# Two heads' scores in one step, compression without zero fills, GLA norm weights applied after the turn

## Chip, cores and metric

The kernel runs on one core of a Trainium2 chip. The metric is the device time of one execution in microseconds; the median of three runs is compared. Engines are named as in the profile: PE is TensorE's matmul, PEld its weight load, DVE VectorE, ACT ScalarE, POOL GpSimd, SP SyncE.

## What is computed

Two transformer blocks, one behind the other, on one sequence of 256 tokens with 1024 channels in fp32. The first block mixes by sparse attention (NSA) and by retention, then an MLP; the second by a state-space scan (SSD) and gated linear attention (GLA), then cross-attention to a memory of 256 rows and a SwiGLU. Cut to what the change touches:

```python
# first block, NSA: 8 heads of 64 in 2 groups, keys compressed in blocks of 32 with stride 16 (15 blocks)
blk = k[cmp_idx] + pe[None, :, None, :]
k_cmp = jax.nn.silu(blk.reshape(n_cmp, G, 32 * 64) @ w1) @ w2          # and v_cmp likewise
p_s = softmax(where(causal, q @ k_sel.T * scale, NEG));  o_s = p_s @ v_sel
p_w = softmax(where(causal, q @ k_win.T * scale, NEG));  o_w = p_w @ v_win
o = gate[..., 0] * o_c + gate[..., 1] * o_s + gate[..., 2] * o_w
# second block, GLA: 4 heads, 256 value channels each
o = rmsnorm_2(o, norm_g).reshape(Bsz, S, GLA_DV)                       # norm_g: 256 weights, same for each head
return (o * jax.nn.silu(r.astype(jnp.float32))).astype(q.dtype)
# second block, SSD: y = C (decay masks) B X, decay masks exp(cs_l - cs_s) per head
```

With 256 tokens all key blocks are selected, so the selected branch and the window branch are both plain causal attention.

## The kernel before

Weights come as 314 units of 128 x 1024 fp32 (512 KB), in the order in which the program asks for them. `load` (line 89 on) issues the transfer on SP's queue into one of 4 `raw` buffers; ACT casts it to fp32r as `wh` (line 96), DVE subtracts to get the low part `wl` (line 97); there are 8 buffers of each. A projection is then three matmuls per 128 channels: high by high, high by low, low by high (`tok_mm` for token rows, `feat_mm` for features). All matmuls go through `mm` (line 106) and all transposes through `tr` (line 110); `split` (line 113) is the cast to a high part on ACT and the subtraction to a low part on DVE.

PSUM has 8 banks in three rings: `acc` with 4, `sm` with 3, `po` with 1. SBUF tiles come from rings too: `k2` (14 buffers) holds most passing tiles, `g2` (9) the gates, values and z tiles.

`stream` is a generator of projections that aren't needed yet; `pump()` takes one piece of it and is called between the steps of the mixers, so that PE has matmuls while other engines do softmax and norms. `need` takes pieces until a result is there. The order of the program isn't the last word: the kernel is built with `schedule_with_timeline_sim=True`, so a planner with a cost for each instruction puts the instructions of each engine in an order ahead of time, and hands out the buffers and banks. On the chip each engine then works through its own list in that order, waiting on semaphores.

The places of the change, in order of time:

- `start` (line 274 on): 14 warm-up matmuls; x's first 128 rows on the SP and ACT queues (line 289); two rows of gains on POOL's queue (line 290), which PE spreads over the partitions by a product with a row of ones, for the first norm (line 318).
- `compress` (line 366 on), called for keys and then for values: four adds put the block positions on (line 374), and for each of four tiles DVE writes zeros twice into a 128-column stationary block (line 381) that takes the high part at columns 0 to 29 and the low part at 64 to 93. 32 matmuls per call, with the weights as the moving side.
- `nsa_rest` (line 610 on): blocks (m, t, i) are pairs of heads by row tile t and group i. `scores` is called for one head at a time: products with the high and the low keys of both branches into one bank, a mask product, the maximum (line 625), two exponentials with their sums (line 629), the reciprocal (631), the gate (633), two scalings (635). `turn` transposes both heads of a block, `values` multiplies with the values. With t = 0 a branch has 128 keys, with t = 1 it has 256.
- `ssd`, `decays` (line 1045 on): POOL makes the block-diagonal tile `bd` (line 1056) that PE spreads over the partitions; ACT takes the exponentials (1061), DVE multiplies with C B (1062). `products` ends a block: sum, z gate (1085), squares on ACT (1087), norm (1089).
- `silu2` (line 461 on) with `mul`: the GLA gate r times its sigmoid, then times the norm weights on POOL (line 469). `gla` (line 1148 on): masks and states, small scalings with the chunk decays (1177, 1178), and for each of four row tiles the norm and the gate (1208), and `to_T`, which transposes a tile and splits it.

Of the kernel before, what the change touches and what calls it, by code (L numbers as in the profile page):

```python
# [32 lines left out]
B_CONV, B_BA, B_DTB, B_AL, B_D, B_A2, B_N = 0, 60, 64, 80, 96, 112, 624  # L33

G_MIX, G_MLP, G_FIN, G_MIX2, G_XATT, G_MEM, G_FFN, G_FIN2, G_SSD, G_GLA, G_NUM = range(11)
# [16 lines left out]
class Builder:  # L52
# [207 lines left out]
    def to_T(self, rows, t, dst, n=8, b0=0):  # L260

        for k0 in range(0, n, 4):
            ps = self.PS()
            for j in range(4):
                self.tr(ps[:, j * P:(j + 1) * P], rows[:, (k0 + j) * P:(k0 + j + 1) * P])
            v = ps.rearrange("p (a b) -> p a b", a=4)
            ts = slice(t * P, (t + 1) * P)
            self.mark = self.split(dst.hi[b0 + k0 // 4][:, :, ts], dst.lo[b0 + k0 // 4][:, :, ts], v)
# [5 lines left out]
    def start(self):  # L274
# [91 lines left out]
    def compress(self, src, pe, w1, w2v, is_v):  # L366

        nc = self.nc
        xt = self.T("k2", [P, 16, 30])
        xv = xt.rearrange("p j (g c) -> p g c j", g=2)  # L370
        sv = src.rearrange("p g (c s) -> p g c s", s=16)
        for h in range(2):
            for g in range(2):
                nc.vector.tensor_tensor(
                    xv[:, g, :, h * 8:(h + 1) * 8], sv[:, g, h:h + 15, 0:16:2],
                    pe[:, None, h * 8:(h + 1) * 8].broadcast_to((P, 15, 8)), op=OP.add)
        xs = []
        for q in range(4):
            x = self.T("k2", [P, 4, P], F32R)
            for c in (30, 94):  # L380
                nc.vector.tensor_scalar(x[:, :, c:c + 34], self.cst[:, None, 0:34].broadcast_to((P, 4, 34)), 0.0, None, op0=OP.mult)
            self.split(x[:, :, 0:30], x[:, :, 64:94], xt[:, 4 * q:4 * q + 4])
            xs.append(x)
        ph = self.PS()
        for q in range(4):
            for j, (wh, wl) in enumerate(self.load(w1, 0, 256, 4 * q, 4)):
                x = xs[q][:, j]
# [3 lines left out]
        hs = self.T("k2", [P, 256])  # L391
        nc.scalar.copy(hs, ph[:, :256])
        pt = self.PS()
        for m in range(2):
            self.mm(pt[:, m * 30:(m + 1) * 30], hs[:, m * P:(m + 1) * P], self.cst[:, C_I94:C_I94 + 30], True, True)
# [65 lines left out]
    def silu2(self, acc, mul=None):  # L461

        out = []
        for t in range(2):
# [3 lines left out]
            if mul is not None:  # L468
                self.nc.gpsimd.tensor_tensor(x, x, mul, op=OP.mult)
# [140 lines left out]
    def nsa_rest(self, kv_, gt, pcT, vbd):  # L610
# [5 lines left out]
        def scores(m, t, i, c):  # L616
            h = 4 * i + 2 * m + c
            w = (t + 1) * P
            ps = self.PS()
            o = ps[:, :2 * w].rearrange("p (a b) -> p a b", a=2)  # L620
            for k in (khi, klo):
                self.mm(o, Q[h // 2][:, c, t * P:(t + 1) * P], k[:, i::2, 0:w], k is khi, False)
            self.mm(o[:, :, t * P:w], self.cb[:, 0], self.cb[:, 1:2].broadcast_to((P, 2, P)), False, True)
            mx = self.S(2)
            nc.vector.tensor_reduce(mx, ps[:, :2 * w].rearrange("p (a b) -> p a b", a=2), axis=AX, op=OP.max, negate=True)  # L625
            e = self.T("k2", [P, 512])
            sm = self.S(2)
            for br in range(2):
                nc.scalar.activation(e[:, br * w:(br + 1) * w], ps[:, br * w:(br + 1) * w], AF.Exp, bias=mx[:, br:br + 1], accum_out=sm[:, br:br + 1])  # L629
            rc = self.S(2)  # L630
            nc.vector.reciprocal(rc, sm)
            f = self.S(2)
            nc.vector.tensor_tensor(f, rc, gt[:, t, h, 1:3], op=OP.mult)
            for br in range(2):
                nc.vector.tensor_scalar(e[:, br * w:(br + 1) * w], e[:, br * w:(br + 1) * w], f[:, br:br + 1], None, op0=OP.mult)
            return e

        def turn(m, t, i, e):


            w = (t + 1) * P
            blocks = [(br, kb) for br in range(2) for kb in range(t + 1)]
            parts = []
            for n in range(t + 1):
                pt = self.PS()
                for a in range(2):
                    br, kb = blocks[2 * n + a]
                    for c in range(2):
                        q = (2 * a + c) * P
                        self.tr(pt[:, q:q + P], e[c][:, br * w + kb * P:br * w + (kb + 1) * P])  # L650
# [331 lines left out]
    def stream2(self, hT, pb, dec, a1T):  # L982
# [28 lines left out]
    def ssd(self, hT, pb, dts, z, dec):  # L1011
# [33 lines left out]
        def decays(g, t, q):  # L1045
# [10 lines left out]
            nc.gpsimd.tensor_tensor(bd, csT[:, t:t + 1].bitcast(F32).broadcast_to((P, 4, P)),  # L1056
# [91 lines left out]
    def gla(self, dec_):  # L1148
# [7 lines left out]
        for i in range(2):  # L1156
# [36 lines left out]
            for t in range(2):  # L1193
# [18 lines left out]
                late = [lambda o=o, t=t, i=i: self.to_T(o, t, yT, 4, i)]  # L1212
# [113 lines left out]
    def block2(self, hT, rest):  # L1326
# [7 lines left out]
        gT = self.gla(dec)  # L1334
# [18 lines left out]
def layout(inp):  # L1353
# [25 lines left out]
    for r in range(3):  # L1379
# [3 lines left out]
        A["gla_b_a_2"][0].reshape(4, P).T, rep(A["ssd_dt_bias_2"]), rep(A["ssd_A_log_2"]), rep(A["ssd_D_2"]), a2], 1)  # L1383
    D["gains"] = np.stack([A["norm_mix"][0], A["norm_mlp"][0], A["norm_final"], A["norm_mix_2"][0], A["norm_xattn_2"][0], A["norm_mem_2"][0],
                           A["norm_ffn_2"][0], A["norm_final_2"], A["ssd_norm_2"][0], np.tile(A["gla_norm_2"][0], 4)])
# [64 lines left out]
```

## Time and profile before

| | |
|---|---|
| median of 3 runs | 1002.63 us (1000.57 to 1003.64) |
| the profiled execution | 1002.8 us, its span 1001.0 us |
| instructions | 16172 |
| busy: PE, DVE, ACT, POOL | 980.6, 661.9, 510.7, 53.8 us |
| mean granted TensorE clock | 0.992 of full speed |
| from HBM | 172.81 MB, 174 GB/s over the span |

The busy shares are means over the whole kernel. Whether a step costs time is read from its own stretch: a table of windows gives, for each, how long each engine was busy, the granted clock and the share of the DMA engines. Rows of the timeline give start, duration, engine, line and operation, the tile written and the tiles read, and in brackets the idle time of the engine before it and what ended it.

### The profile page before, as it was taken

The numbers are of one execution on the slowest core, as the hardware profiler recorded it, in microseconds if no ns is written. First come the engines' busy times: TensorE is split into PE (matmuls) and PEld (weight loads), VectorE is DVE, ScalarE is ACT, GpSimd is POOL, SyncE is SP. The second block draws the span as 40 slices with busy tenths as digits, with TensorE's granted clock in tenths as the row PEclk, the third lists the DMA queues.
The fourth block names the chain that finished last, engine by engine and source line by source line (L and its number), as shares of the span: only waits on it lengthen the run. The fifth ranks groups of instructions, "written<-read, shape, count | busy, mean of one in ns | idle before, by whom it ended". The sixth has DMA issues, their size and how long they took to land.

```text
span 1001.0 us, 16172 instructions
## 1 busy us (share of the span) xinstructions
PE 980.6 (98%) x6388; PEld 876.9 (88%) x6388; DVE 661.9 (66%) x994; ACT 510.7 (51%) x797; POOL 53.8 (5%) x80
## 2 busy tenths in 40 slices
PE   8999999899999999999999989999999999999997
PEld 5878999787888899789898888998998879899995
DVE  6798768866755555678878666677756467455543
ACT  5656546635644444465765535555545345444432
POOL 1000100000000000100010231200000000000000
PEclk8999999999999999999999999999999999999999
DMA  7656744233655666276446442753755157556531
GB/s 274 213 195 223 253 138 146 87 128 126 221 190 185 200 215 195 106 251 199 155 147 190 148 148 85 253 191 128 229 190 187 45 190 248 193 169 203 177 126 42
DMA packets 49212, 174.92 MB, mean 175 GB/s; under 512 B 5984, under 2 KB 6240, under 8 KB 49136
## 3 DMA queue, kind: packets, MB, share of 16 engines
q1 hardware_dynamic: 46512, 166.15, 50.5%
q0 software_dynamic: 2192, 6.94, 2.2%
q8 instruction: 50, 0.82, 0.3%
q10 hardware_dynamic: 432, 0.79, 0.2%
q14 instruction: 26, 0.21, 0.1%
HBM read 172.81 MB, written 1.05 MB: 174 GB/s over the span
## 4 chain that ended last, share of the span: by engine, by line
PE 90%; DVE 5%; ACT 2%; DMA 2%; issue 1%; POOL 0%; POOLq 0%; ACTq 0%; DVEq 0%
PE acc L106 64%; PE sm L106 23%; PE sm L110 2%; DVE wl L97 2%; PE po L106 1%; DMA raw<-in_wbig_dram 1%; ACT wh L96 1%; DMA k<-in_gains_dram 1%; ACT hh L113 0%; DVE hl L113 0%; ACT k L629 0%; DVE k L113 0%; DVE gd L555 0%; DVE sc L625 0%; PE po L110 0%
## 5 line engine op out<-in xcount | busy, mean ns | idle before, releaser
L97 DVE TENSOR_TENSOR wl<-raw,wh 128x1024 fp32r<-128x1024 f32 (+1 forms) x314 | 379.5, 1221 | 214.7 <-ACT wh L96 213.4
L96 ACT CAST wh<-raw 128x1024 fp32r<-128x1024 f32 (+1 forms) x314 | 325.5, 1049 | 292.7 <-PE acc L106 133.7
L106 PE MATMUL acc<-hh,wh 128*128 128x256 f32 x736 | 207.2, 283 | 3.8 <-ACT g L271 3.3
L106 PE MATMUL acc<-hh,wl 128*128 128x256 f32 x736 | 207.5, 282 | 0.0
L106 PE MATMUL acc<-hl,wh 128*128 128x256 f32 x736 | 206.4, 281 | 0.0
L106 PE MATMUL acc<-wl,hh 128*128 128x512 f32 (+1 forms) x400 | 158.1, 396 | 0.7 <-DVE wl L97 0.7
L106 PE MATMUL acc<-wh,hh 128*128 128x512 f32 (+1 forms) x400 | 156.7, 397 | 1.2 <-ACT hh L113 1.1
L106 PE MATMUL acc<-wh,hl 128*128 128x512 f32 (+1 forms) x400 | 156.4, 396 | 0.0
L106 PEld LDWEIGHTS acc<-hh,wh 128*128 128x128 f32 x736 | 138.4, 189 | 5.4 <-ACT g L271 3.5
L106 PEld LDWEIGHTS acc<-hl,wh 128*128 128x128 f32 x736 | 139.1, 189 | 0.2
L106 PEld LDWEIGHTS acc<-hh,wl 128*128 128x128 f32 x736 | 139.0, 189 | 0.3 <-issue 0.2
L106 PE MATMUL sm<-hh,wl 128*128 128x256 f32 x488 | 136.5, 280 | 0.0
L106 PE MATMUL sm<-hl,wh 128*128 128x256 f32 x488 | 136.4, 279 | 0.0
L106 PE MATMUL sm<-hh,wh 128*128 128x256 f32 x488 | 136.4, 279 | 0.0
L106 PEld LDWEIGHTS sm<-hl,wh 128*128 128x128 f32 x488 | 91.7, 188 | 0.8
L106 PEld LDWEIGHTS sm<-hh,wh 128*128 128x128 f32 x488 | 91.4, 187 | 0.9
L106 PEld LDWEIGHTS acc<-wh,hh 128*128 128x128 f32 x400 | 75.7, 190 | 18.6 <-ACT hh L113 2.7
L106 PEld LDWEIGHTS acc<-wl,hh 128*128 128x128 f32 x400 | 76.0, 190 | 18.2 <-DVE wl L97 1.9
L106 PEld LDWEIGHTS sm<-hh,wl 128*128 128x128 f32 x488 | 91.6, 188 | 0.0
L106 PEld LDWEIGHTS acc<-wh,hl 128*128 128x128 f32 x400 | 75.9, 190 | 17.9 <-DVE hl L113 1.1
L106 PE MATMUL acc<-wl,gd 128*128 128x512 f32 x216 | 85.4, 396 | 0.0
L106 PE MATMUL acc<-wh,gd 128*128 128x512 f32 x216 | 85.1, 395 | 0.0
(292 smaller groups left out, 1079.4 us busy)
## 6 DMA issues: line engine op xcount, KB each, us to landing
raw<-in_wbig_dram SPq DMA_DIRECT2D x311, 512.0 KB, 4.1
k<-in_gains_dram POOLq DMA_DIRECT2D x18, 256.0 KB, 4.5
k<-in_mem_dram POOLq DMA_DIRECT2D x4, 256.0 KB, 5.6
raw<-in_wbig_dram SPq DMA_DIRECT2D x2, 420.0 KB, 3.8
k<-in_decay_dram POOLq DMA_DIRECT2D x4, 192.0 KB, 5.1
xr<-in_x_dram SPq DMA_DIRECT2D x1, 512.0 KB, 6.6
out_dram<-k SPq DMA_DIRECT2D x2, 256.0 KB, 2.5
out_dram<-k ACTq DMA_DIRECT2D x2, 256.0 KB, 2.7
```

The source lines that it names most:

```text
L96: nc.scalar.copy(wh[:, :m], raw[:, :m])
L97: nc.vector.tensor_sub(wl[:, :m], raw[:, :m], wh[:, :m].bitcast(F32))
L106: self.nc.tensor.matmul(out, lhsT, rhs, start=start, stop=stop)
L110: self.nc.tensor.transpose(out, src, self.ident[:n, :n])
```

## The change

- `start`: the two gain rows go from POOL's queue to ACT's, behind ACT's half of x.
- `compress`: one tile with 32 instead of 30 columns per group of rows, its two spare columns zeroed by one small memset; two adds instead of four; no zero fills. The stationary block has 96 columns: high, low, high. ACT writes high twice with one instruction, DVE the low part. The product that adds high and low part up takes 96 rows instead of 128.
- `scores` takes both heads of a pair. With t = 0 both heads and both branches share one bank, one mask product, one maximum and one product with the scale; with t = 1 each head has its own bank and its own mask product and the four scalings stay. Reciprocal and gate are one instruction each per pair. The two pumps that stood behind each head now stand behind the pair.
- `decays`: `bd` is made by DVE instead of POOL.
- GLA norm weights: the product on POOL and the two transfers of gains fall away; the weights lie as two columns of 128 in the parameter tile, and `to_T` puts them on as it splits the turned rows, in two halves, each with one instruction on ACT and one on DVE.

```diff
-    def to_T(self, rows, t, dst, n=8, b0=0):
+    def to_T(self, rows, t, dst, n=8, b0=0, gain=None):
...
-            self.mark = self.split(dst.hi[b0 + k0 // 4][:, :, ts], dst.lo[b0 + k0 // 4][:, :, ts], v)
+            hi, lo = dst.hi[b0 + k0 // 4], dst.lo[b0 + k0 // 4]
+            if gain is None:
+                self.mark = self.split(hi[:, :, ts], lo[:, :, ts], v)
+                continue
+
+            for a in range(2):
+                h, l, u, g = hi[:, a::2, ts], lo[:, a::2, ts], v[:, a::2], gain[:, a:a + 1]
+                self.nc.scalar.activation(h, u, AF.Copy, scale=g)
+                self.nc.vector.scalar_tensor_tensor(l, u, g, h.bitcast(F32), op0=OP.mult, op1=OP.subtract)
...
-            nc.gpsimd.dma_start(rows[q], d["gains"][G_MIX:G_MIX + 1, q * 512:(q + 1) * 512])
+        for q in range(2):
+            nc.scalar.dma_start(rows[q], d["gains"][G_MIX:G_MIX + 1, q * 512:(q + 1) * 512])
...
-        xt = self.T("k2", [P, 16, 30])
-        xv = xt.rearrange("p j (g c) -> p g c j", g=2)
+        xt = self.T("k2", [P, 16, 32])
+        nc.vector.memset(xt[:, :, 30:32], 0.0)
+        xv = xt[:, :, 0:30].rearrange("p j (g c) -> p g c j", g=2)
         sv = src.rearrange("p g (c s) -> p g c s", s=16)
         for h in range(2):
-            for g in range(2):
-                nc.vector.tensor_tensor(
-                    xv[:, g, :, h * 8:(h + 1) * 8], sv[:, g, h:h + 15, 0:16:2],
-                    pe[:, None, h * 8:(h + 1) * 8].broadcast_to((P, 15, 8)), op=OP.add)
+            nc.vector.tensor_tensor(
+                xv[:, :, :, h * 8:(h + 1) * 8], sv[:, :, h:h + 15, 0:16:2],
+                pe[:, None, None, h * 8:(h + 1) * 8].broadcast_to((P, 2, 15, 8)), op=OP.add)
         xs = []
         for q in range(4):
-            x = self.T("k2", [P, 4, P], F32R)
-            for c in (30, 94):
-                nc.vector.tensor_scalar(x[:, :, c:c + 34], self.cst[:, None, 0:34].broadcast_to((P, 4, 34)), 0.0, None, op0=OP.mult)
-            self.split(x[:, :, 0:30], x[:, :, 64:94], xt[:, 4 * q:4 * q + 4])
+
+            x = self.T("k2", [P, 4, 3, 32], F32R)
+            v = xt[:, 4 * q:4 * q + 4]
+            nc.scalar.copy(x[:, :, 0::2], v[:, :, None, :].broadcast_to((P, 4, 2, 32)))
+            nc.vector.tensor_sub(x[:, :, 1], v, x[:, :, 0].bitcast(F32))
             xs.append(x)
...
-                self.mm(ph[:, :256], x, wh, q + j == 0, False)
-                self.mm(ph[:, :256], x, wl, False, q + j == 6)
+                self.mm(ph[:96, :256], x, wh, q + j == 0, False)
+                self.mm(ph[:96, :256], x, wl, False, q + j == 6)
...
-            if mul is not None:
-                self.nc.gpsimd.tensor_tensor(x, x, mul, op=OP.mult)
...
+        def scores(m, t, i):
+
+            h0, w = 4 * i + 2 * m, (t + 1) * P
+            n = 2 // (t + 1)
+            mx, sm = self.S(4), self.S(4)
+            banks, e = [], []
+            for c0 in range(0, 2, n):
+                ps = self.PS()
+                v = ps.rearrange("p (c b w) -> p c b w", c=n, b=2)
+                for c in range(n):
+                    for k in (khi, klo):
+                        self.mm(v[:, c], Q[(h0 + c0 + c) // 2][:, (c0 + c) % 2, t * P:(t + 1) * P], k[:, i::2, 0:w], c == 0 and k is khi, False)
+                self.mm(v.rearrange("p c b w -> p (c b) w")[:, :, t * P:w], self.cb[:, 0], self.cb[:, 1:2].broadcast_to((P, 2 * n, P)), False, True)
+                nc.vector.tensor_reduce(mx[:, 2 * c0:2 * (c0 + n)], ps.rearrange("p (a w) -> p a w", w=w), axis=AX, op=OP.max, negate=True)
+                banks.append(ps)
+                e.append(self.T("k2", [P, 2 * n, w]))
+            for a in range(4):
+                b, x = divmod(a, 2 * n)
+                nc.scalar.activation(e[b][:, x], banks[b][:, x * w:(x + 1) * w], AF.Exp, bias=mx[:, a:a + 1], accum_out=sm[:, a:a + 1])
+            rc = self.S(4)
             nc.vector.reciprocal(rc, sm)
+            f = self.S(4)
+            nc.vector.tensor_tensor(f.rearrange("p (a b) -> p a b", a=2), rc.rearrange("p (a b) -> p a b", a=2), gt[:, t, h0:h0 + 2, 1:3], op=OP.mult)
+            if t == 0:
+                nc.vector.tensor_tensor(e[0], e[0], f[:, :, None].broadcast_to((P, 4, P)), op=OP.mult)
+            else:
+                for a in range(4):
+                    nc.vector.tensor_scalar(e[a // 2][:, a % 2], e[a // 2][:, a % 2], f[:, a:a + 1], None, op0=OP.mult)
...
-                es[n] = []
-                for c in range(2):
-                    es[n].append(scores(*blocks[n], c))
-                    self.pump()
-            else:
+                es[n] = scores(*blocks[n])
                 self.pump()
+            self.pump()
...
-        gg = self.gain(G_GLA)
         for i in range(2):
-            yield from self.s_tok(f"r{i}", w, 4608 + i * 512, 512, hT, lambda acc, i=i: self.silu2(acc, gg[i]))
+            yield from self.s_tok(f"r{i}", w, 4608 + i * 512, 512, hT, self.silu2)
...
-            nc.gpsimd.tensor_tensor(bd, csT[:, t:t + 1].bitcast(F32).broadcast_to((P, 4, P)),
+            nc.vector.tensor_tensor(bd, csT[:, t:t + 1].bitcast(F32).broadcast_to((P, 4, P)),
...
-                late = [lambda o=o, t=t, i=i: self.to_T(o, t, yT, 4, i)]
+                late = [lambda o=o, t=t, i=i: self.to_T(o, t, yT, 4, i, gain)]
```

## Rows read from the trace of the kernel before

**Rows 1.** The page's first part: busy time, share of the span, instructions.
```profile
PE 980.6 (98%) x6388; PEld 876.9 (88%) x6388; DVE 661.9 (66%) x994; ACT 510.7 (51%) x797; POOL 53.8 (5%) x80
```
**Rows 2.** Windows: stretch, length, each engine's busy time, granted clock, DMA share, GB/s.
```profile
0.00:12.06 12.06, 9.61 (x26) 3.88 (x26) 4.78 (x14) 3.94 (x6) 2.47 (x8) 0.87 0.88 315
...
67.60:70.45 2.85, 0.51 (x4) 0.20 (x3) 2.79 (x7) 1.77 (x4) 0.00 (x0) 0.97 0.47 165
70.45:73.70 3.25, 3.25 (x8) 2.60 (x9) 2.88 (x5) 0.00 (x0) 0.00 (x0) 0.50 0.61 178
183.30:203.00 19.70, 16.55 (x118) 13.68 (x117) 15.37 (x45) 10.69 (x35) 1.14 (x2) 1.00 0.17 54
...
480.00:580.00 100.00, 100.00 (x673) 89.51 (x672) 77.32 (x103) 62.67 (x112) 12.96 (x12) 1.00 0.50 162
590.90:594.42 3.52, 0.23 (x2) 0.02 (x1) 2.96 (x5) 2.15 (x4) 0.56 (x1) 1.00 0.56 159
594.42:599.40 4.98, 4.98 (x29) 4.98 (x30) 1.37 (x2) 0.00 (x0) 0.00 (x0) 0.66 0.64 203
```
**Rows 3.** Timeline of the start: start, duration, engine, line, what, idle before.
```profile
1.23 5.25 PE L106 MATMUL po<-k 128*128 128x512 bf16 x14 [1.23 <-DVE k L280]
...
1.94 1.01 POOL L290 DMA_DIRECT2D k<-in_gains_dram  x2
...
7.70 1.09 PE L106 MATMUL po<-k,k 1*128 1x512 f32 x2 [1.23 <-DMA k<-in_gains_dram]
```
**Rows 4.** The page's DMA issues: queue, count, KB each, median us to landing.
```profile
k<-in_gains_dram POOLq DMA_DIRECT2D x18, 256.0 KB, 4.5
...
out_dram<-k ACTq DMA_DIRECT2D x2, 256.0 KB, 2.7
```
**Rows 5.** Timeline of DVE and ACT about the compression.
```profile
60.56 1.17 DVE L381 TENSOR_SCALAR k<-cst 128x136 fp32r<-128x136 f32 x8
...
67.23 1.05 ACT L96 CAST wh<-raw 128x1024 fp32r<-128x1024 f32 x1 [1.70 <-PE acc L106]
...
68.84 0.42 DVE L113 TENSOR_TENSOR hl<-sm,hh 128x256 fp32r<-128x256 f32 x1
69.18 1.22 DVE L97 TENSOR_TENSOR wl<-raw,wh 128x1024 fp32r<-128x1024 f32 x1
```
**Rows 6.** PE's wait in the last score blocks; lines 635 and 629 by source.
```profile
184.69 0.35 PE L106 MATMUL sm<-hh,gd 128*128 128x256 f32 x1 [0.94 <-DVE k L113]
...
L635 DVE TENSOR_SCALAR k<-k,sc x32: 275/314/353, 155.3 to 197.7; 128x128 f32<-128x128 f32 x16, 128x256 f32<-128x256 f32 x16
...
L629 ACT ACTIVATE k<-sm,sc x32: 357/421/477, 153.9 to 196.5; 128x128 f32<-128x128 f32 x16, 128x256 f32<-128x256 f32 x16
```
**Rows 7.** SSD by line: durations ns min/median/max, first and last start.
```profile
L1056 POOL TENSOR_TENSOR k<-ropec,cst x8: 1036/1046/2133, 482.6 to 570.2; 128x512 fp32r<-128x512 f32 x8
...
L1062 DVE TENSOR_TENSOR k<-k,cbt x7: 679/691/1145, 508.5 to 576.4; 128x512 f32<-128x512 f32 x7
```
**Rows 8.** Timeline ahead of GLA, and line 1178 by source.
```profile
584.03 5.04 POOL L469 TENSOR_TENSOR g<-g,k 128x512 f32<-128x512 f32 x4 [2.40 <-DMA k<-in_gains_dram]
...
585.28 1.33 DVE L1178 TENSOR_SCALAR k<-gd,gdec 128x64 f32<-128x64 f32 x1
...
587.13 0.73 DVE L1177 TENSOR_SCALAR k<-gd,gdec 128x64 f32<-128x64 f32 x1
587.79 1.34 DVE L1178 TENSOR_SCALAR k<-gd,gdec 128x64 f32<-128x64 f32 x1
...
593.78 0.59 ACT L271 ACTIVATE g<-acc 128x512 f32<-128x512 f32 x1
...
L1178 DVE TENSOR_SCALAR k<-gd,gdec x4: 248/788/1337, 585.3 to 613.0; 128x64 f32<-128x64 f32 x4
```
**Rows 9.** Chain of waits: start, length, matmuls of 256 columns in a row.
```profile
74.51 2.40 PE sm L106 x20
...
258.85 5.65 PE sm L106 x48
```

More of the change, by code (lines that the diff above doesn't have):

```diff
@@ L31 @@
 A_PEK, A_PEV, A_CK2, A_CV2, A_N = 0, 16, 32, 288, 416
-B_CONV, B_BA, B_DTB, B_AL, B_D, B_A2, B_N = 0, 60, 64, 80, 96, 112, 624
-G_MIX, G_MLP, G_FIN, G_MIX2, G_XATT, G_MEM, G_FFN, G_FIN2, G_SSD, G_GLA, G_NUM = range(11)
+B_CONV, B_BA, B_DTB, B_AL, B_D, B_A2, B_GG, B_N = 0, 60, 64, 80, 96, 112, 624, 626
+G_MIX, G_MLP, G_FIN, G_MIX2, G_XATT, G_MEM, G_FFN, G_FIN2, G_SSD, G_NUM = range(10)
 BUFS = dict(
@@ L386, in compress @@
             for j, (wh, wl) in enumerate(self.load(w1, 0, 256, 4 * q, 4)):
-                x = xs[q][:, j]
-                self.mm(ph[:, :256], x, wh, q + j == 0, False)
-                self.mm(ph[:, :256], x, wl, False, q + j == 6)
+                x = xs[q][:, j].rearrange("p a b -> p (a b)")
+                self.mm(ph[:96, :256], x, wh, q + j == 0, False)
+                self.mm(ph[:96, :256], x, wl, False, q + j == 6)
             self.pump()
-        hs = self.T("k2", [P, 256])
-        nc.scalar.copy(hs, ph[:, :256])
+        hs = self.T("k2", [96, 256])
+        nc.scalar.copy(hs, ph[:96, :256])
         pt = self.PS()
         for m in range(2):
-            self.mm(pt[:, m * 30:(m + 1) * 30], hs[:, m * P:(m + 1) * P], self.cst[:, C_I94:C_I94 + 30], True, True)
+            self.mm(pt[:, m * 30:(m + 1) * 30], hs[:, m * P:(m + 1) * P], self.cst[:96, C_I94:C_I94 + 30], True, True)
         th = self.T("cbt", [P, 60], bufs=2)
@@ L459, in keep, with silu2 @@
         return out
-    def silu2(self, acc, mul=None):
+    def silu2(self, acc):
         out = []
@@ L614, in nsa_rest @@
         nT = self.newT(1)
[L616 to L630, printed above, removed]
-            nc.vector.reciprocal(rc, sm)
[L632 to L636, printed above, removed]
@@ new lines, in scores @@
+        def scores(m, t, i):
[17 more added lines that the diff above has]
+            rc = self.S(4)
+            nc.vector.reciprocal(rc, sm)
+            f = self.S(4)
[5 more added lines that the diff above has]
+                    nc.vector.tensor_scalar(e[a // 2][:, a % 2], e[a // 2][:, a % 2], f[:, a:a + 1], None, op0=OP.mult)
+            return lambda c, br, kb: e[(2 * c + br) // (2 * n)][:, (2 * c + br) % (2 * n), kb * P:(kb + 1) * P]
@@ L638, in turn @@
         def turn(m, t, i, e):
-            w = (t + 1) * P
             blocks = [(br, kb) for br in range(2) for kb in range(t + 1)]
@@ L649, in turn @@
                         q = (2 * a + c) * P
-                        self.tr(pt[:, q:q + P], e[c][:, br * w + kb * P:br * w + (kb + 1) * P])
+                        self.tr(pt[:, q:q + P], e(c, br, kb))
                 x = [self.T("k2", [P, 512], F32R) for _ in range(2)]
@@ L1146, in gla_decays, with gla @@
         return res
-    def gla(self, dec_):
+    def gla(self, dec_, gain):
         nc = self.nc
@@ L1333, in block2 @@
         sT = self.ssd(hT, pb, dts, z, dec)
-        gT = self.gla(dec)
+        gT = self.gla(dec, pb[:, B_GG:B_GG + 2])
         mix = self.gated("ab", hT, sT, "u_ssd", 8, gT, "u_gla", 8)
@@ L1382, in layout @@
         np.ascontiguousarray(conv.reshape(5, 12, P).transpose(2, 1, 0)).reshape(P, 60),
-        A["gla_b_a_2"][0].reshape(4, P).T, rep(A["ssd_dt_bias_2"]), rep(A["ssd_A_log_2"]), rep(A["ssd_D_2"]), a2], 1)
+        A["gla_b_a_2"][0].reshape(4, P).T, rep(A["ssd_dt_bias_2"]), rep(A["ssd_A_log_2"]), rep(A["ssd_D_2"]), a2, A["gla_norm_2"][0].reshape(2, P).T], 1)
     D["gains"] = np.stack([A["norm_mix"][0], A["norm_mlp"][0], A["norm_final"], A["norm_mix_2"][0], A["norm_xattn_2"][0], A["norm_mem_2"][0],
-                           A["norm_ffn_2"][0], A["norm_final_2"], A["ssd_norm_2"][0], np.tile(A["gla_norm_2"][0], 4)])
+                           A["norm_ffn_2"][0], A["norm_final_2"], A["ssd_norm_2"][0]])
     D.update(constants())
@@ L1403, in constants @@
     c[:30, C_I94:C_I94 + 30] = np.eye(30)
-    c[64:94, C_I94:C_I94 + 30] = np.eye(30)
+    c[32:62, C_I94:C_I94 + 30] = np.eye(30)
     for r in range(3):
```

## Prediction

> **What bounds the kernel now.** I read the page's busy shares first, then a table of windows, then the chain of waits, and only then the timeline of the four places where the table shows a hole. TensorE (PE) is busy 98% of the span [rows 1], and in a long stretch such as 480 to 580 us it has no hole at all [rows 2]. So an edit that takes work off VectorE (DVE), ScalarE (ACT) or GpSimd (POOL) gains nothing where PE streams, and no edit here takes matmul columns away: the score products keep their columns, the masks of two heads become one instruction over the same columns, and the compression still moves 256 columns per matmul. What can be won is PE's idle time and the half clock behind it. The windows show four holes: the start (12.06 us to the first projection matmul, PE busy 9.61 of it with warm-up, gains and transposes); 67.60 to 70.45, PE busy 0.51 of 2.85; the last score blocks, 183.30 to 203.00, PE busy 16.55 of 19.70; and 590.90 to 594.42, PE busy 0.23 of 3.52 [rows 2]. Behind the second and the fourth, the granted clock is 0.50 and 0.66 of full speed, so 1.2 GHz instead of 2.4 GHz for much of a stretch [rows 2]. The tail after the last matmul isn't touched.
>
> **Part 1, the gains at the start.** PE finishes its 14 warm-up matmuls at 1.23 + 5.25 = 6.48 and stands until 7.70 for the two gain rows, issued from POOL at 1.94 [rows 3]. They move to the ACT queue, behind one half of x. A transfer from ACT takes 2.7 us to land, the gains from POOL 4.5 [rows 4]. Even issued at 2.5 (an estimate: behind POOL's old time) they land by 5.2, before the warm-up ends, so warm-up becomes the late one. ACT issues two more transfers ahead of its table load; its first large step waits for x, which covers them; without that cover the price would be the 1.01 us that POOL spends on the same two [rows 3]. Everything up to the first projection hangs on that product, so I take the whole wait, **-1.2 us**; ends 0 (a weight tile is late instead, DMA being 88% busy there [rows 2]) and -1.2.
>
> **Part 2, compression.** The 16 zero fills go, eight of them as one block of 1.17 us at 60.56 [rows 5], ahead of a hole in which DVE is busy 2.79 of 2.85 us [rows 2]. The adds go from four to two per call and a small memset comes; I set that at nothing, a few tenths at most either way. ACT's copies write more elements (256 for 120); they lie ahead of a cast that waits at 67.23 for PE [rows 5], which is their cover. In the hole PE waits first for the subtraction at 68.84 (it frees a PSUM bank), then for the low half of a weight unit, 69.18 to 70.40 [rows 5]. With the fills gone the first comes at about 67.7. The second can't come 1.17 earlier: the cast of that unit runs from 67.23 to 68.28 [rows 5], so the subtraction ends at about 68.3 + 1.2 = 69.5, which is 0.9 ahead of today. The weight is late next, and PE's idle time shrinks from 2.34 (2.85 - 0.51) to about 1.4. Does the clock still fall? PE stood 0.94 us at 184.69 [rows 6], where the clock stayed full; it stood 2.34 here and 3.29 (3.52 - 0.23) in the fourth hole, and behind both it fell [rows 2]. The estimate of 1.4 is nearer to the first, so I take it as kept: eight matmuls in 3.25 us at half clock [rows 2] would take half, a further 1.6. Together **-2.5 us**; ends 0 and -3.9 (the hole gone altogether: 2.3 + 1.6).
> The stationary block of these 64 matmuls shrinks from 128 to 96 columns. They start 0.120 us apart (20 in 2.40), as other 256-column matmuls do (48 in 5.65, 0.118 us) [rows 9], so the moving side sets the pace and I take nothing; if the pace went with the stationary columns, it would be 64 x 0.120 / 4 = 1.9 us. The Trainium skill, TensorE: Matmul & The Clock Gate, section on LDWEIGHTS, says that a load's time goes by its columns; by that rule alone the sum would have 64 x 32 / 1.2 ns = 1.7 us less (an estimate from that page). No row shows a shorter load.
>
> **Part 3, scores of two heads at a time.** While the stream of other matmuls lasts it covers every latency here (two pumps per block, as before, though both now come behind the pair). It has nearly run out by 183, and there PE waits for DVE and ACT, 0.94 for a PSUM bank at 184.69 the longest [rows 6], of 3.15 idle in all (19.70 - 16.55 [rows 2]). In the four blocks of the first row tile the pair needs one score bank instead of two, one wide maximum, one reciprocal and one product; four scalings of at least 0.275 us [rows 6] become one product over 512 columns, 0.68 [rows 7]. So the bank wait should go: -0.9, and some -0.4 of DVE time with it. The Trainium skill, VectorE: DVE Perf Modes, section "The perf-mode tier table", speaks against that edit: an fp32 scaling in SBUF runs at twice the rate of a two-tensor product. By its cycles alone four blocks would cost 4 x (512 - 256) / 0.96 ns = 1.1 us more on VectorE (an estimate from that page); at 128 columns the row's 0.275 us is mostly not column time, and the measurement decides. In the four blocks of the second row tile both heads' four exponentials (some 0.42 us each [rows 6]) stand ahead of the first scaling, where today the first head is done early. The last block is on the way to PE's next work with nothing beside it: I take half of two exponentials, +0.4. Together **-0.9 us**; ends -3.1 (all idle time gone) and +3.4 (four blocks, each two exponentials later).
>
> **Part 4, the decay masks' product from POOL to DVE.** Eight of them, 1.04 us each on POOL [rows 7]; on DVE 0.68 each (a two-input product of this shape), so 5.4 us more of DVE work. DVE is busy 77.3 of 100 us there and PE has no hole [rows 2]; besides, the same DVE product takes up to 1.145 beside POOL instead of 0.68 [rows 7], which comes back. The new wait is what counts: the product needs a free buffer, and on DVE it holds up what is queued behind it, the low halves of weights above all, on which PE waits in turn. I take **0**: 22.7 us of free DVE time in the window [rows 2] covers 5.4. Ends: -0.5 (half a bank wait of rows 6, no row being nearer) and +5.4, each product in full.
>
> **Part 5, GLA norm weights.** POOL's four products go (584.03 to 589.07, 5.04 us [rows 8]), and with them two gain transfers and their wait. The chain of waits through the fourth hole runs on DVE and ACT: the last SSD block's steps stand on DVE behind small scalings (64 columns) at 585.28, 587.13 and 587.79 that take 1.33, 0.73 and 1.34 us beside the POOL products, where the shortest of their kind takes 0.248 [rows 8]. Alone they would be 3.40 - 3 x 0.25 = **2.6 us** shorter. Behind them comes ACT's square of that block, which frees a buffer, and then the tanh at 593.78 [rows 8], which needs the buffer and frees the bank that PE stands for. Moved up by 2.6, the tanh runs at about 591.2 and PE idles some 0.7; the clock then has less cause to fall than at the 0.94 of Part 3. The price of its fall here: 29 matmuls in 4.98 us, where 0.118 each would be 3.4 [rows 2, 9], so 1.6. Together **-4.2 us**; ends 0 and -4.9 (3.29 + 1.6). The weights come back in the turned rows' split, as two halves on ACT and two on DVE, four times; three lie behind a pump and the next tile's products, the last behind the whole SSD up-projection. If that cover were gone it would be one added instruction per engine and turn, about 0.3 us each (from the shortest rows of 6 and 8).
>
> **Sum.** -1.2 - 2.5 - 0.9 + 0 - 4.2 = -8.8. From the profiled execution's own 1002.8 (span 1001.0) that is 994.0. The median of the runs shown is 1002.63, 0.2 lower, so 993.8; the times below count from that median too.
>
> **Rivals.** (a) The fourth hole stays. The bank waits for a buffer that the last SSD block frees; if the plan of the new kernel puts other work ahead of that block on DVE (it already puts GLA scalings there), the wait keeps its size. For it: nothing in the code ties the order. Against: the work ahead gets shorter. Then -1.2 - 2.5 - 0.9 = -4.6: 998.0. (b) The holes fill again. The order on each engine is planned anew, PE still waits for the same number of buffers and banks, and what is saved on DVE shows as idle time there. Then only the start remains: 1001.4. (c) Slower: the decay products on DVE. If each is issued behind a weight subtraction of 1.22 us [rows 5] while PE has reached the matmul that wants it, each costs 1.22 + 0.68 = 1.9 us, eight 15.2, and with the -8.8 of the rest the time is 1009.0. It decides from about 1.5 us per product (12 us in all, 3 more than the rest gives); against it stands PE without a hole in that window.
>
> **How the numbers follow.** Forecast 0.60, (a) 0.20, (b) 0.13, (c) 0.07. Measurement tells some 0.3%, 3 us, from no change: faster means below 999.6. Forecast and nearly all of (a) lie there: 0.79; (b) with the rest 0.14; (c) 0.07. The range goes down to 988.5: parts 2, 3 and 5 have 1.4, 2.2 and 0.7 left to their good ends and the stationary columns 1.9, 6.2 in all, and I reach 5.3 of it. It goes up to 1000.5, past (a), and leaves out most of (b) and (c).
>
> **What would show it.** Right: the first projection matmul at about 10.9; no window at half clock near 70 or 595; PE idle under 1 us where the bank wait was; no POOL product over 0.7 us. Wrong: PE waiting for a mask product in the SSD, the tanh before GLA still late, or a new hole with a half-clock stretch behind it anywhere; one such stretch costs 1.6, two undo part 2.

## The result, and the profile after

The changed kernel takes 995.65 us (992.33 to 996.93, 6 runs) and the kernel before, on the same chip, 1001.85 (1000.07 to 1003.64): a ratio of 0.9933, with an interval of 0.9913 to 0.9953, so some 6.5 us faster. The profiled execution of after took 996.21 us, its span is 994.4 against 1001.0.

The page's first part for after, the line that answers to [rows 1]:

```profile
PE 975.6 (98%) x6384; PEld 876.1 (88%) x6384; DVE 657.4 (66%) x956; ACT 511.4 (51%) x801; POOL 35.3 (4%) x64
```

PE is again busy for all but some 19 us. POOL lost 18.5 us of work, DVE 4.5, and PE hardly any instruction: the gain must lie in PE's idle time, in its clock, or in something that this line doesn't show. The table of windows of after, over the places where [rows 2] had holes (columns as there):

```profile
0.00:11.32 11.32, 9.25 (x26) 4.12 (x27) 4.44 (x14) 3.94 (x6) 1.46 (x6) 0.92 0.86 316
66.00:70.90 4.90, 2.82 (x13) 1.83 (x12) 4.78 (x9) 1.93 (x4) 0.00 (x0) 1.00 0.33 110
70.90:74.30 3.40, 3.40 (x11) 2.67 (x10) 1.59 (x2) 0.26 (x1) 0.00 (x0) 0.50 0.78 255
193.30:197.20 3.90, 2.30 (x15) 1.67 (x16) 2.94 (x10) 2.79 (x9) 0.94 (x2) 1.00 0.43 134
197.20:200.60 3.40, 3.40 (x18) 3.40 (x18) 1.27 (x3) 0.48 (x1) 0.00 (x0) 0.50 0.03 5
588.20:590.20 2.00, 0.34 (x4) 0.14 (x2) 1.74 (x3) 1.93 (x4) 0.55 (x1) 1.00 0.00 0
590.20:599.00 8.80, 7.78 (x78) 7.31 (x78) 4.63 (x9) 3.47 (x6) 0.00 (x0) 1.00 0.41 121
```

The hole of the compression is still there, and in this execution the half clock (0.50, so 1.2 GHz) behind it too. The last score blocks have a half clock that before didn't have. Only the hole ahead of GLA became smaller, and the clock behind it stayed at 2.4 GHz, where [rows 2] had 0.66.

Next come landmarks that both kernels have: the start of the same matmul in the two timelines, and the length of each stretch between them.

| stretch, by PE's landmarks | before, us | after, us | difference |
|---|---|---|---|
| start to the first projection | 12.06 | 11.32 | -0.74 |
| to the first compression product | 62.28 | 62.47 | +0.19 |
| to the last product of the sparse attention (scores) | 127.70 | 127.46 | -0.23 |
| to the first product of the second block that reads tile ropes | 279.75 | 278.22 | -1.53 |
| to the first turn of the next norm (over GLA) | 194.11 | 191.82 | -2.29 |
| to the end | 325.12 | 323.14 | -1.98 |

Some 3.5 us of 6.6 come from two long stretches, 202 to 482 us and 676 us to the end, in which the change edits nothing on PE's way. No step of the prediction speaks of them. The first two stretches move without any edit, too: ten of the kernels timed here have the instructions of before in the same order on every compute engine up to the first compression product, and their traces reach it between 71.25 and 74.34 us.

### The profile page after: what moved, and what is told of

It is laid out like the page before. It is cut to its first block, busy times and chain, and to the rows that moved or that the text cites. A ratio compares the mean times of both kernels' runs of the same rounds, so it can differ in the third digit from the quotient of the medians.

```text
span 994.4 us, 16103 instructions
## 1 busy us (share of the span) xinstructions
PE 975.6 (98%) x6384; PEld 876.1 (88%) x6384; DVE 657.4 (66%) x956; ACT 511.4 (51%) x801; POOL 35.3 (4%) x64
## 4 chain that ended last, share of the span: by engine, by line
PE 93%; DVE 2%; DMA 2%; ACT 1%; issue 1%; SPq 0%; POOLq 0%; DVEq 0%; ACTq 0%
PE acc L106 66%; PE sm L106 23%; PE sm L110 2%; PE po L106 2%; DMA raw<-in_wbig_dram 1%; DVE wl L97 1%; DMA posi<-in_pos_dram 1%; ACT wh L96 0%; ACT hh L113 0%; DVE gd L563 0%; PE po L110 0%; DVE k L365 0%; DVE hl L113 0%; DVE k L444 0%; DVE k L651 0%
## 5 line engine op out<-in xcount | busy, mean ns | idle before, releaser
L106 PE MATMUL acc<-wh,k 128*128 128x512 f32 x216 | 84.7, 397 | 0.0
```

The lines of the kernel that those rows point to most:

```text
L106: self.nc.tensor.matmul(out, lhsT, rhs, start=start, stop=stop)
```

## The experiments

Each was timed in five rounds beside the kernel before on the same chip. The first four put one part of the change alone into the kernel before.

**GLA part alone** (norm weights in the parameter tile and in the turned rows' split, POOL's products gone).

```diff
-B_CONV, B_BA, B_DTB, B_AL, B_D, B_A2, B_N = 0, 60, 64, 80, 96, 112, 624
+B_CONV, B_BA, B_DTB, B_AL, B_D, B_A2, B_GG, B_N = 0, 60, 64, 80, 96, 112, 624, 626
...
-                late = [lambda o=o, t=t, i=i: self.to_T(o, t, yT, 4, i)]
+                late = [lambda o=o, t=t, i=i: self.to_T(o, t, yT, 4, i, gain)]
```

> The kernel before with the GLA norm weights alone moved to the turned rows. Theory: of the 6 us that the whole change gave, about half comes from here. The four POOL products go, the small scalings take 0.25 us instead of up to 1.3, the hole of PE ahead of GLA falls from 3.3 us to about 1.7, and no stretch at half clock follows (1.6): -3.2 us against the kernel before. Rival (the hole is set by the order on ACT and by the free buffer alone, the gain came from elsewhere): hole over 3 us, half clock behind it, 0 +- 0.5 us.

Measured: 995.08 us, ratio 0.9931 (0.9919 to 0.9943). This part alone gives all that the whole change gives, twice the 3.2 us of its theory. What the theory said of the hole came (PE stands 1.68 us for the tanh, and the granted clock is 1.00 from 588 to 600 us), so the other half comes from elsewhere.

**Scores alone, compression alone, masks' product on DVE alone** (`nc.gpsimd` to `nc.vector` in one line; the other two are the change's hunks).

> The kernel before with the scores of two heads in one step alone. Theory: the wait for a PSUM bank in the last score blocks (0.94 us) goes, but in the last block both heads' four exponentials stand ahead of the first scaling, so PE idles over 1 us ahead of the last transposes and the clock falls behind it (1.6 us): 0 to +1.5 us. Rival (the forecast's part 3, the bank wait counts and the tail costs 0.4): -0.9 us, no half clock near 197.

> The kernel before with the compression without zero fills alone. Theory: DVE is 1.2 us ahead by 62 us, but PE's hole at 67 to 71 is set by the weight unit whose cast ACT takes up at 67 to 68 and by DVE's order; it keeps 2 us and the half clock behind it: -0.5 to +0.3 us. Rival (forecast's part 2): the hole shrinks to 1.4 us and the clock stays, -2.5 us.

> The kernel before with the SSD mask product alone moved from POOL to DVE. Theory: eight products of 0.68 us lie in DVE's free time, PE has no wait in the SSD: 0 +- 0.5 us. Rival (c of the prediction): PE waits for mask products, over 3 us slower.

Measured: 1001.67, 1000.79 and 1001.63 us; ratios 0.9997 (0.9986 to 1.0008), 0.9999 (0.9986 to 1.0011) and 0.9998 (0.9988 to 1.0009). None of the three moves the time by more than the 1.4 us that these intervals leave open. For the masks that was the forecast. For the scores the theory held, half clock included; windows about the last turn, scores alone, then the masks' part alone, whose scores are those of before:

```profile
195.50:199.50 4.00, 3.90 (x20) 3.90 (x21) 2.26 (x5) 1.05 (x2) 0.00 (x0) 0.57 0.06 20
```
```profile
195.50:199.50 4.00, 3.53 (x29) 3.29 (x30) 3.09 (x7) 1.73 (x4) 0.00 (x0) 1.00 0.43 131
```

For the compression the waits of PE tell why; timelines of the kernel with the compression part alone (first two rows) and of the one with the masks' part alone, which has the compression of before:

```profile
67.44 0.44 PE L110 MATMUL sm<-cst,k 128*128 128x128 f32 x2 [0.87 <-DVE hl L113]
...
69.17 0.50 PE L106 MATMUL acc<-wl,hh 128*128 128x512 f32 x1 [1.29 <-DVE wl L97]
```
```profile
68.59 0.44 PE L110 MATMUL sm<-cst,k 128*128 128x128 f32 x2 [1.79 <-DVE hl L113]
...
69.72 0.50 PE L106 MATMUL acc<-wl,hh 128*128 128x512 f32 x1 [0.69 <-DVE wl L97]
```

Without the zero fills the first wait is 0.9 shorter and the second 0.6 longer: 2.16 against 2.48 us of idle time in all. The second wait is 0.69 in all ten traces with the compression of before and 1.29 or 1.30 in all four without zero fills. The half clock of the theory didn't come: behind both of these holes PE ran at a granted 1.00 from 70 to 76 us. Behind after's 0.78 + 1.30 = 2.08 it ran at 0.50, so the clock isn't tied to that size. Nor is it to the program: of the ten traces with the compression of before, idle 1.96 to 2.94 us there, five show the half clock behind the hole ([rows 2] is one of them, with 2.34) and five, up to 2.48, don't.

**What the GLA part does outside GLA.** The mean distance of two 256-column matmuls' starts is 117.3 ns in the kernel before and in the three kernels that gain nothing, and 116.9 in the GLA part alone and in after. The GLA part adds two columns to the parameter tile par, and by that moves every tile behind it in SBUF, the weight tiles wh and wl among them, by 32 bytes (the two columns are 8; the moves given here are those of the layout, no trace shows an address). Four kernels test this by unused columns alone:

```diff
-B_CONV, B_BA, B_DTB, B_AL, B_D, B_A2, B_N = 0, 60, 64, 80, 96, 112, 624
+B_CONV, B_BA, B_DTB, B_AL, B_D, B_A2, B_N = 0, 60, 64, 80, 96, 112, 626
```

(640 instead of 626 in the second and, put onto the GLA part, in the third; in the fourth par stays, and the tile of ones ahead of hh, hl and g2 grows by 32 bytes, which moves those and all behind them.)

> The kernel before with two unused columns on the parameter tile par (624 to 626, as the change makes it): every tile allocated behind it (raw, the weight tiles wh and wl, ropec, gd) moves up by 32 bytes in SBUF, no instruction of the compute engines is added, removed or moved. Theory L (the addresses of the operands set a part of the matmul pace, and that is what half of the GLA part's gain is): the mean start-to-start of 256-column matmuls falls from 117.3 to 116.9 ns as in the kernel with the GLA part alone, and the time falls by about 3 us (ratio 0.997), the hole at 588 us staying at 3.45. Rival W (the pace follows the work that the GLA part takes off POOL and DVE): pace 117.3, ratio 1.000.

> The kernel before with 16 unused columns on par (624 to 640): the same tiles move by 64 bytes, so wh, wl and gd keep a start of 32 modulo 64. Theory L, if the start modulo 64 bytes is what counts: pace 117.3 ns and ratio 1.000. If any move counts (another modulus, or a chance arrangement): the pace is a third value. Rival W: 117.3, ratio 1.000.

> The GLA part alone with par at 640 columns instead of 626: its weights and its two removed POOL passes as before, but wh, wl and gd again at 32 modulo 64 as in the kernel before. Theory L: pace back to 117.3 ns, the gain falls from 6.5 to about 3.5 us (ratio 0.9965). Rival W: pace 116.9 and ratio 0.993 as without the padding.

> The kernel before with the tile of ones widened by 32 bytes: here the stationary operands' tiles hh and hl and also g2 move to 0 modulo 64, and wh, wl, gd too. Theory L in the form that the weights' own start counts: pace 116.9 ns, ratio 0.997. In the form that it is the place of the weights against hh and hl (both at 32 before, 32 and 0 in the kernel with the GLA part): pace 117.3, ratio 1.000. Rival W: 117.3, ratio 1.000.

Measured: 999.18 us, ratio 0.9975 (0.9960 to 0.9991); 1005.37, 1.0041 (1.0025 to 1.0056); 1002.26, 1.0007 (0.9991 to 1.0023); 999.91, 0.9982 (0.9962 to 1.0001). Kernels with the same instructions on every compute engine differ by 6.2 us, by unused columns alone, and the GLA part with 640 columns has no gain left to show. Theory L holds, rival W falls. Its detail, the start modulo 64, falls too: 624 and 640 columns agree in it, and 640 is slower. The kernel with the wider tile of ones decides between neither form of its theory: its distances are 117.2 ns (256 columns), near the second form's 117.3, and 232.7 (512), near the 232.5 that goes with the first. The rows by tile show it where all kernels do the same work, from the last product of the tile acc with wh and hl to the last with wh and gd (duration min/median/max, then first and last start in us). In order: before, before with 626, before with 640, GLA part alone (626), GLA part with 640:

```profile
L106 PE MATMUL acc<-wh,hl x400: 287/394/632, 13.1 to 829.5; 128*128 128x512 f32 x129, 128*128 128x280 f32 x5
L106 PE MATMUL acc<-wh,gd x216: 387/393/500, 265.8 to 993.2; 128*128 128x512 f32 x108
```
```profile
L106 PE MATMUL acc<-wh,hl x400: 287/395/628, 13.1 to 828.2; 128*128 128x512 f32 x129, 128*128 128x280 f32 x5
L106 PE MATMUL acc<-wh,gd x216: 389/389/499, 265.3 to 990.5; 128*128 128x512 f32 x108
```
```profile
L106 PE MATMUL acc<-wh,hl x400: 289/389/628, 12.4 to 828.7; 128*128 128x512 f32 x129, 128*128 128x280 f32 x5
L106 PE MATMUL acc<-wh,gd x216: 389/397/497, 262.6 to 994.0; 128*128 128x512 f32 x108
```
```profile
L106 PE MATMUL acc<-wh,hl x400: 287/395/628, 12.3 to 822.9; 128*128 128x512 f32 x129, 128*128 128x280 f32 x5
L106 PE MATMUL acc<-wh,gd x216: 387/389/496, 263.4 to 985.2; 128*128 128x512 f32 x108
```
```profile
L106 PE MATMUL acc<-wh,hl x400: 289/389/793, 11.2 to 826.1; 128*128 128x512 f32 x129, 128*128 128x280 f32 x5
L106 PE MATMUL acc<-wh,gd x216: 389/397/504, 263.1 to 991.4; 128*128 128x512 f32 x108
```

The stretch takes 163.7, 162.3, 165.3, 162.3 and 165.3 us: it goes by the width of par, with or without the GLA part. So the GLA part's own gain is read at one width, over the stretch from the ropes product to the next norm's turn: 195.26 to 191.83 with 626 columns (-3.4), 197.35 to 194.33 with 640 (-3.0).

**Two more widths of par, with the GLA part.** 656 columns move the tiles by 128 bytes, 648 by 96.

> The GLA part alone with par at 656 columns: the tiles behind it move by 128 bytes, so each has the same place modulo 128 as in the kernel before. If the place modulo 128 is what counts, the pace is the kernel before's (256 columns 117.3 ns, 512 columns 233.3), and the time shows what the GLA part gives without the shift of addresses: at the two other places its own gain was 4.1 us (995.1 against 999.2) and 3.1 us (1002.3 against 1005.4), so 997.5 to 998.6, ratio 0.996 to 0.997. If the address itself counts and not its place modulo 128, the pace is another one and the time is open.

> The GLA part alone with par at 648 columns: the tiles behind it at the fourth place, 0 modulo 128 (32, 64 and 96 are measured). Theory of a place modulo 128: a fourth pair of paces, between those seen (256 columns 116.9 to 119.75 ns, 512 columns 229.6 to 233.3), time 994 to 1003. If only the place modulo 64 counted, it would be the pace of 626 columns (116.9 and 232.5) and 995.1; but 624 and 640 columns, which agree modulo 64, gave 117.3 and 119.75, which speaks against this.

Measured: 992.64 us, ratio 0.9917 (0.9903 to 0.9931), and 1000.85, 0.9995 (0.9984 to 1.0006). The theory of a place modulo 128 falls with the first: its time was to be 997.5 to 998.6, and its distances are 116.7 (256 columns) and 230.8 ns (512) where the kernel before has 117.3 and 233.3. It fits one stretch only, over GLA (190.85 us, which is before's 194.11 less the GLA part's 3.0 to 3.4). The second lies within what was expected, a fourth pair of distances (118.3 and 232.4), and speaks once more against a place modulo 64, which would have given 995.1 us. So the same edit takes 992.64 to 1002.26 us by the width of par alone.

**The second half's scores apart, the square off ACT**, both in the changed kernel and at its addresses. The scores' edit keeps the pairs for t=0 and calls the score function of before, one head at a time, for t=1.

```diff
-            nc.scalar.activation(z[t][g], yv, AF.Square, accum_out=ssq)
+            if g == 1 and t == 1:
+                nc.vector.tensor_tensor(z[t][g], yv, yv, op=OP.mult)
+                nc.vector.tensor_reduce(ssq, z[t][g], axis=AX, op=OP.add)
+            else:
+                nc.scalar.activation(z[t][g], yv, AF.Square, accum_out=ssq)
```

> The changed kernel with two edits in two stages: in the second row half (t=1) the two heads' scores stand apart again, each with its own maxima, exponentials and scalings, while the first half keeps the pairs; and the square ahead of the last SSD norm is made on DVE (product and sum) instead of ACT. Theory on the scores: the hole of 1.15 us at 195.11 and the half clock of 197.2 to 200.6 come of the pair's chain of one maxima row, four exponentials and four scalings in front of the turn, so both go and the last score product comes about 2 us earlier against the changed kernel (0.8 is what the pairs gave there). Rival: the tail drains anyway, and the last score product does not move. Theory on the GLA hole: the tanh that releases PE at 590.18 waits in ACT's queue behind the square and the weight cast, so without the square (0.81 us) the hole of 1.8 us falls to about 1.1. Rival: the cast or its buffer is what is late, the hole stays 1.8. Sum by the theories 992.5 to 993.5; by the rivals 995.6.

Measured: 992.69 us, ratio 0.9917 (0.9904 to 0.9931). The score stretch takes 125.67 us against after's 127.46 and before's 127.70, without a half clock, as its theory said. First after, then this kernel, PE's long wait and windows of the tail:

```profile
195.11 0.98 PE L110 MATMUL sm<-cst,k 128*128 128x128 f32 x4 [1.15 <-DVE k L651]
```
```profile
190.00:194.00 4.00, 3.29 (x25) 2.62 (x24) 3.25 (x13) 2.91 (x11) 1.14 (x2) 1.00 0.00 0
194.00:198.00 4.00, 3.69 (x31) 3.45 (x32) 2.80 (x6) 1.41 (x3) 0.00 (x0) 1.00 0.38 135
```

So the pairs gain 2.0 us in the first half and lose 1.8 in the second. At the GLA hole the theory was wrong and the rival right; timelines of after, then of this kernel:

```profile
587.03 1.05 ACT L96 CAST wh<-raw 128x1024 fp32r<-128x1024 f32 x1 [4.81 <-PE acc L106]
...
587.98 0.62 ACT L1098 ACTIVATE g<-k 128x512 f32<-128x512 f32 x1
...
588.61 1.03 ACT L96 CAST wh<-raw 128x1024 fp32r<-128x1024 f32 x1
...
589.54 0.59 ACT L279 ACTIVATE g<-acc 128x512 f32<-128x512 f32 x1
...
590.18 0.38 PE L106 MATMUL acc<-hh,wh 128*128 128x256 f32 x1 [1.66 <-ACT g L279]
```
```profile
583.84 1.05 ACT L96 CAST wh<-raw 128x1024 fp32r<-128x1024 f32 x1 [4.81 <-PE acc L106]
...
585.25 1.04 ACT L96 CAST wh<-raw 128x1024 fp32r<-128x1024 f32 x1 [0.36 <-PE acc L106]
...
586.20 0.59 ACT L279 ACTIVATE g<-acc 128x512 f32<-128x512 f32 x1
...
586.84 0.38 PE L106 MATMUL acc<-hh,wh 128*128 128x256 f32 x1 [1.52 <-ACT g L279]
```

Without the square the second weight cast waits for PE, which frees its tile as it runs dry; the tanh that PE needs stands behind that cast in ACT's order. The time lies within the theories' sum (992.5 to 993.5) all the same, and that is luck: the first 74 us, in which nothing is edited, are 1.4 us shorter here than in after, within the spread of 3.1 us that this stretch shows by itself.

**That cast on DVE, the second half's scores apart, and 656 columns**, in the changed kernel.

```diff
-        nc.scalar.copy(wh[:, :m], raw[:, :m])
+        (nc.vector.tensor_copy if i == 191 else nc.scalar.copy)(wh[:, :m], raw[:, :m])
```

> The changed kernel with three edits: the second row half's scores apart as in the run before (the square back on ACT), the weight cast that stands ahead of the tanh at the GLA hole made by DVE instead of ACT, and par at 656 columns (the addresses at which the kernel with the GLA part alone took 992.6 instead of 995.1 us). Theory on the hole: since the square on DVE moved nothing (1.68 us left), it is the cast, which starts only when PE's last product frees its tile, plus the tanh behind it; without the cast the hole falls by about 0.6 to 1.0 us, to 0.7 to 1.1. Rival: DVE's rounding remainder of the load before becomes what PE waits for, the hole stays 1.5 to 1.8. Theory on the addresses: the pace of this kernel is that of the GLA part alone at 656 columns (256 columns 116.67 ns, 512 columns 230.8), the time 989.5 to 991; rival: the pace is bound to each kernel's stream and is again that of 626 columns (116.93 and 232.5), the time 992 to 993.

Measured: 988.55 us, ratio 0.9886 (0.9868 to 0.9904), the fastest of all. Both theories hold: PE's wait for the tanh is 0.92 us, and the distances are 116.4 and 230.7 ns. The time came out 1 us below the 989.5 to 991 that was expected.

```profile
580.70 1.05 ACT L96 CAST wh<-raw 128x1024 fp32r<-128x1024 f32 x1 [4.76 <-PE acc L106]
...
581.65 0.62 ACT L1129 ACTIVATE g<-k 128x512 f32<-128x512 f32 x1
...
582.40 0.60 ACT L279 ACTIVATE g<-acc 128x512 f32<-128x512 f32 x1
...
582.93 0.69 DVE L96 CAST wh<-raw 128x1024 fp32r<-128x1024 f32 x1
...
583.05 0.38 PE L106 MATMUL acc<-hh,wh 128*128 128x256 f32 x1 [0.92 <-ACT g L279]
```

## Why the prediction came out right, and where its steps did not

The time (993.8 forecast, 995.65 measured) was right, but in part by luck, not by the prediction's own terms. Those give -4.2 in place of -8.8; the other -2.4 is what the moved tiles give alone, which no step named. Signs that the prediction had listed for being wrong came as well: a half clock near 70 us, a new one at 197, and a tanh ahead of GLA for which PE still stands 1.66 us. (The kernel before with 626 columns differs from before by -1.63, +1.15 and -1.88 us over the last three stretches of the table, -2.4 in all. After's own share is what is left: +0.1, -3.4 and -0.1, beside -0.74, +0.19 and -0.23 ahead of them. All these are single executions.)

**Part 1, the start: -1.2 forecast, -0.74 measured.** The wait for the gains is gone, as said, and the warm-up is late next. The step that failed is the cover of what follows it; timeline of after:

```profile
6.71 1.12 PE L106 MATMUL sm<-k,k 1*128 1x512 f32 x2
...
6.91 1.23 DVE L97 TENSOR_TENSOR wl<-raw,wh 128x1024 fp32r<-128x1024 f32 x1 [1.11 <-ACT wh L96]
...
8.05 0.74 DVE L327 SCALAR_TENSOR_TENSOR g<-xr,sc,sm 128x512 f32<-128x512 f32 x1
...
9.53 1.97 PE L110 MATMUL sm<-cst,g 128*128 128x128 f32 x8 [0.84 <-DVE g L327]
```

With the gains early, a weight subtraction of 1.23 us stands on DVE ahead of the norm, and PE waits 0.84 for it. But ten kernels with the instructions of before up to there, without this edit, reached their first projection between 10.50 and 12.80 us (the GLA part alone at 11.32, the masks alone at 10.83), so even -0.74 is not shown to be this edit's; it wasn't run alone. And [rows 4] was read for the wrong transfers: its 4.5 us belong to eighteen of 256 KB, while the trace of before gives 5.5 for the two rows of 2 KB.

**Part 2, the compression: -2.5 forecast, nothing measured (alone -1.4 to +1.1 us).** "The weight is late next" was right. But 0.6 of the 0.9 us taken from the bank's wait came back there: in after two casts of ACT wait 2.09 us for DVE, and the weight's cast, at 67.23 before [rows 5], starts behind them.

```profile
67.51 0.71 ACT L561 CAST gd<-sm 128x256 fp32r<-128x256 f32 x2 [2.09 <-DVE gd L563]
...
68.12 1.05 ACT L96 CAST wh<-raw 128x1024 fp32r<-128x1024 f32 x1
...
70.06 0.49 PE L106 MATMUL acc<-wl,hh 128*128 128x512 f32 x1 [1.30 <-DVE wl L97]
```

The clock's term, 1.6, was read from two holes of one execution. The runs break that reading: clock kept behind 2.48 us of idle time, fallen behind 2.08, and in half of ten traces there was no half clock to win back. As for the narrower stationary block, 16 matmuls take 1.88 us at 76.95 in after's chain of waits, 0.118 each, as with 128 columns [rows 9]:

```profile
76.95 1.88 PE sm L106 x16
```

The loads did become shorter. Those of the first of the two calls, before, then after:

```profile
L106 PEld LDWEIGHTS sm<-wh,k x16: 187/188/193, 74.1 to 78.7; 128*128 128x128 f32 x16
```
```profile
L106 PEld LDWEIGHTS sm<-wh,k x15: 160/161/276, 74.0 to 78.3; 128*96 128x96 f32 x15
```

That is 27 ns less for 32 columns, but each load runs beside the matmul before it (in after one at 76.79 us, between the matmul starts 76.71 and 76.91), and the starts stay 0.118 apart. The rule on load time by columns in the Trainium skill, TensorE: Matmul & The Clock Gate, section on LDWEIGHTS, is borne out by this trace for the load itself; the 1.7 us estimated from it would have needed loads that nothing covers.

**Part 3, the scores: -0.9 forecast, -0.2 measured.** The bank wait went, and the kernel with pairs in the first half alone gained 2.0 over the stretch. The step that failed is "+0.4, half of two exponentials" for the second half: its price was 1.8. The wait behind the last scalings is 1.15 us, but it is the half clock of 3.4 us behind it that costs most, half of its length, 1.7, and I had listed a new half clock only among the signs of failure, not as a term. The rule of the Trainium skill (VectorE: DVE Perf Modes, section "The perf-mode tier table"), by whose cycles alone the product in place of four scalings costs more on DVE, doesn't decide at this size: the product takes 0.684 us in after, four scalings of at least 0.275 took 1.1 [rows 6]. Most of a scaling isn't column time: 0.275 with 128 columns, 0.346 with 256 in after.

**Part 4, the masks: 0 forecast, 0 measured.** Eight products of 0.68 us, and PE waits for none.

**Part 5, GLA: -4.2 forecast, -3.0 to -3.4 measured.** The mechanism is the forecast one. In after the small scalings take 0.24 to 0.25 us instead of up to 1.34 [rows 8], the tanh comes earlier, and the clock stays up:

```profile
L1188 DVE TENSOR_SCALAR k<-gd,gdec x4: 243/244/247, 584.0 to 607.2; 128x64 f32<-128x64 f32 x4
```

The term that was mis-sized is the hole's: 1.6 us gone (PE idle 3.29 before, 1.66 after), not 2.6, since ACT's own order (cast, square, cast, tanh) becomes the limit, and its second cast can't start before PE runs dry. The clock's 1.6 came as said, although those 1.66 us stayed. Seven traces without the GLA part stand 3.18 to 3.88 us there, and six of them have the half clock behind it; seven with it stand 0.92 to 1.68, and none has. The one that hasn't, the kernel with the wider tile of ones, kept the clock behind a hole of the old size, so the hole's length alone doesn't decide:

```profile
591.99 0.38 PE L106 MATMUL acc<-hh,wh 128*128 128x256 f32 x1 [3.27 <-ACT g L271]
```
```profile
588.00:600.00 12.00, 8.61 (x85) 7.86 (x83) 7.27 (x12) 4.88 (x10) 0.56 (x1) 1.00 0.46 139
```

Of the rivals, (c) is excluded by the masks alone. (b), holes that fill again, describes the compression and the second half's scores, not GLA. What (a) feared, other work ahead of the tanh, happened on ACT and not on DVE, and took 1.0 of the hole's 2.6, not all.

## What to carry to other kernels

Before a gain is put down to an edit, repeat the kernel before with the edit's memory footprint alone: here unused columns, with no other edit, moved the time by -2.5 to +3.7 us, as much as the edit itself, and the ten traces alike up to the compression differ by 3.1 us there, so a stretch in which the clock may fall shows little below that in one execution. When a wait is taken away, walk every engine's own order up to the next late step, ACT's casts too; they gave back 1.0 of 2.6 us at GLA and 0.6 of 0.9 at the compression. A pair that shortens the work where PE streams lengthens it where the stream runs out, so choose the form block by block.

## What the runs showed of the hardware that was not expected

The distance between matmuls with the same shapes, clock and work depends on where the tiles lie in SBUF. Mean start-to-start of consecutive matmuls over the whole trace, stalls left out, and the time of the identical stretch behind 829.5 us in before:

| kernel | tiles moved by | 256 columns, ns | 512 columns, ns | stretch, us |
|---|---|---|---|---|
| before (624) | 0 | 117.3 | 233.3 | 163.7 |
| before, 626 | 32 bytes | 116.9 | 232.5 | 162.3 |
| GLA part, 626 | 32 | 116.9 | 232.5 | 162.3 |
| after (626) | 32 | 116.9 | 232.5 | 162.3 |
| before, 640 | 64 | 119.8 | 229.6 | 165.3 |
| GLA part, 640 | 64 | 119.8 | 229.6 | 165.3 |
| GLA part, 648 | 96 | 118.3 | 232.4 | 163.6 |
| GLA part, 656 | 128 | 116.7 | 230.8 | 163.3 |
| last kernel, 656 | 128 | 116.4 | 230.7 | 163.2 |
| before, ones wider | 32, hh, hl and g2 too | 117.2 | 232.7 | 163.3 |

Kernels with the same addresses agree to 0.3 ns, whatever their other edits. The two shapes don't move together: 64 bytes cost the 256-column matmuls 2.5 ns and gave the 512-column ones 3.7. Nor do matmuls of one shape that read different tiles. At moves of 0, 32, 64, 96 and 128 bytes the 512-column distances of wh with hh, which lies ahead of par, are 233.4, 233.3, 228.0, 233.2 and 229.4 ns; those of wh with gd, which moves with wh, are 232.3, 227.6, 233.4, 228.8 and 232.2. Which rule the addresses follow stays open: the place modulo 64 and modulo 128 were both tried and both fell. Between 626 and 656 columns with the GLA part, 2.4 us, the edit is the same: the stretches of the scores and up to the ropes product, with PE's idle time alike to 0.1 us, are 0.9 and 1.0 us shorter with 656. The kernel before with 656 columns wasn't run, so what the GLA part itself gives there is open.
